# Fixing the order of an expert down stage: even turns of slots and chunks, earlier loads, halves set apart

## The chip, the cores and the metric

The kernel runs on one core of a Trainium2 chip. The metric is the device time of one execution in microseconds (us), as a median of three. All times inside the execution are counted from the start of its profiled span. TensorE is called PE, VectorE DVE, ScalarE ACT; SP is the queue that issues nearly all loads.

## The reference, cut to what matters

Two transformer blocks on 256 tokens of width 1024, all in float32. The stage that changes lies on the seam between them: the down projection of 16 experts (32 tokens each), their gated sum into the residual, and the first feed-forward network of the second block (width 2816), which needs the norm of that residual.

```python
y = jnp.einsum('becf,efd->becd', hid, w_down) * gate[..., None]
x = x + jnp.zeros_like(h).at[bidx, idx].add(y)          # end of block one
# block two, first layer:
h = x + 0.5 * swiglu(rms_norm_2(x, ffn1_norm[0]), ffn1_gate[0], ffn1_up[0], ffn1_down[0])
```

## The kernel before, in words

Activations are kept transposed, as `xt`: eight chunks of 128 features by 256 tokens. The expert down projection goes by **slots**: slot c makes chunk c of the residual. In a slot, eight `y` steps (16 matmuls each, one weight tile of 1 MB each, `in_wd`) make four groups of four experts; each group is copied from PSUM by ACT (`ys`, L1299) and scattered onto the tokens by one `moe` matmul (`sc`, L1304). After the fourth, DVE adds the sum to the residual (`x`, L1310) and ACT and DVE split the chunk into a high and a low part (`xs`), since weights and activations are multiplied as three fp32r products (`mm3`, L478 to L480).

The scale of the norm is a factor per token, so the gate and up projections can begin before the norm is known: as soon as chunk c of the residual is there, 22 **units** (`u`, c, j) multiply it with its rows of the gate and up weights, six matmuls each, and add the result to a partial sum `Pt` (copied by ACT for c = 0, L1323, added by DVE after, L1325). Chunk 7's units come in `first_ffn` (`gate_up`), where the norm's scale (`fin1`, `fin2`, the chain of small DVE operations L561 and L466 to L473) is applied to `Pt` (`evac`) and the down matmuls follow (`down`, `dn`).

The units' weights come in three tiles a chunk (`in_f0g` twice 1 MB for eight units each, `in_f0h` 0.75 MB for six). Each is split on chip in two column halves: ACT writes `wh` (L401), DVE writes `wl` (L402). `slices()` (L306) gives the order of `y`, `sc`, `x` and units: units begin two `y` steps (`LAG`) into slot 1 and are spread over the steps. The same list sets the order of the loads: a unit weight stands `EARLY` = 2 `y` tiles ahead of the step that needs it. `pump` (L376) issues loads while buffers are free: four `raw` ones, and those of a `ring` of 17 that `hold` leaves. The ring also holds the residual, `xs` (two), `Pt` (six), the expert outputs (two) and a pair for each split weight. PSUM tiles of units rotate over the three banks of `pb`.

The order in which instructions stand on an engine is made by a scheduler that goes by priority and its own estimates; only where `behind` binds two instructions is their order fixed. In this stage before, nothing binds them.

Of the kernel before, what the change touches and what calls it, by code (L numbers as in the profile page):

```python
# [32 lines left out]
NF = 22  # L33
RING, RAW, T1, T2 = 17, 4, 10, 10
WARM = (12, 32)
LAG, EARLY = 2, 2
# [202 lines left out]
def _body(tc, nc, const, ringp, work, psum, a, out):  # L239
# [3 lines left out]
    st = {"turn": 0, "ring": 0, "raw": 0, "next": 0, "hold": 0, "la": 2, "late": 0, "gate": None}  # L243
# [62 lines left out]
    def slices():  # L306
# [15 lines left out]
        yield sc  # L322
        yield ("x", 7)
        yield from units[n:]
# [17 lines left out]
    for j in range(NF):  # L342
        if j % 8 == 0:
            add_gs(7, j // 8)
        if j >= 3 and (j - 3) % 2 == 0:
            d0 += add(a["ffn1d0"][len(d0):len(d0) + 1], 1, 1)
    d0 += add(a["ffn1d0"][len(d0):11], 11 - len(d0), 1)
# [28 lines left out]
    def pump():  # L376
        while st["next"] < len(stream):
            if st["raw"] < RAW:
                fetch()
            elif not kinds[st["next"]] and st["ring"] + 2 * any(kinds[i] for i in raw) < RING - st["hold"]:  # L380
# [96 lines left out]
    def mm3(ps, wh, wl, x, first, last):  # L477
        PE.matmul(ps, lhsT=wl, rhs=x[:, 1], start=first, stop=False, skip_group_check=True)  # L478
        PE.matmul(ps, lhsT=wh, rhs=x[:, 0], start=False, stop=False, skip_group_check=True)  # L479
        PE.matmul(ps, lhsT=wh, rhs=x[:, 1], start=False, stop=last, skip_group_check=True)  # L480
# [7 lines left out]
    class Parts:  # L488


        def __init__(self, name):
            self.half = [ralloc([128, 4, 2, 256], F32R, name) for _ in range(2)]

        def __getitem__(self, c):
            return self.half[c // 4][:, c % 4]
# [7 lines left out]
        def part(self, k, c, n):  # L503
            h = self.half[c // 4]
# [12 lines left out]
    class Norm:  # L517


        def __init__(self, g, parts=True, late=0):  # L520
# [3 lines left out]
            if parts:  # L524
                self.x = Parts("xs")
# [53 lines left out]
        def free(self):  # L579
            rfree(2)  # L580
# [501 lines left out]
    n2 = Norm(None, parts=False)  # L1082
# [181 lines left out]
    def slice_steps():  # L1264


        norm, Pt, py, ys, macc = None, [], {}, {}, {}

        def unit(c, j):
# [11 lines left out]
        for op in slices():  # L1281
            if op[0] == "y":
# [5 lines left out]
                w = raw[k].rearrange("p (k g n) -> p k g n", k=4, g=4)  # L1288
                for c in range(4):
                    for g in range(4):  # L1290
                        e = 4 * q + g
                        h = HT[e // 8][:, e % 8].rearrange("p h j s -> p (h j) s")
                        PE.matmul(py[s, q][32 * g:32 * g + 32], lhsT=h[:, 4 * i + c], rhs=w[:, c, g],  # L1293
                                  start=i == 0 and c == 0, stop=i == 1 and c == 3, skip_group_check=True,
                                  tile_position=(0, 32 * g))
                done(k)
                if i == 1:
                    ys[s, q] = t1("ys")[:, :128]
                    S.activation(ys[s, q], py.pop((s, q)), AF.Copy)  # L1299
            elif op[0] == "sc":  # L1300
                _, s, q = op
                if q == 0:
                    macc[s] = pa("moe", (128, 256))
                PE.matmul(macc[s], lhsT=ys.pop((s, q)), rhs=SC[q // 2][:, q % 2],  # L1304
                          start=q == 0, stop=q == 3, skip_group_check=True)
            elif op[0] == "x":
                c = op[1]
                if norm is None:
                    norm = Norm(vc("ffn1n", 0, 8))
                V.tensor_tensor(xt[:, c], macc[c], xt[:, c], op=OP.add)  # L1310
                norm.chunk(c)
                if c == 0:
                    st["hold"], st["la"], st["late"] = 6, 1, 0
                if c == 7:
                    rfree(2)
            else:
                _, c, j = op
                p = unit(c, j)
                if c == 0:
                    if j % 4 == 0:  # L1320
                        Pt.append(ralloc([128, 4, 2, 256], F32, "Pt"))
# [398 lines left out]
```

## Time and profile before

| what | value |
|---|---|
| median of three executions | 1592.27 us (1589.86 to 1592.68) |
| the profiled execution, its own time | 1591.57 us |
| its span | 1589.8 us |
| PE busy | 1445.0 us, 91% of the span |
| DVE busy | 949.6 us, 60% |
| ACT busy | 660.6 us, 42% |
| mean bandwidth of loads | 252 GB/s |

Busy time of PE is modelled, since matmuls overlap; the distance from one matmul's start to the next says more. A window gives its length, the busy time of PE, PE's weight loads (PEld), DVE, ACT and GpSimd (POOL) with their instructions, the granted share of PE's full clock (2.4 GHz), the busy share of the DMA engines, and GB/s. The span has stages: up to 200 us the first mixer, to 474 us the expert gate and up projections, which load 1 MB tiles without a break, from 474 to 729 us the slots, to 820 us the first feed-forward network, and then dense stages of the second block.

### The profile page before, as it was taken

What the parts mean: (1) busy time and instruction counts of PE and PEld (TensorE: products, weight loads), DVE (VectorE), ACT (ScalarE), POOL (GpSimd) and SP (SyncE); (2) the same over time, 40 slices, a digit from 0 to 9 for tenths busy, and PEclk for the clock granted to TensorE, in tenths of its full rate; (3) what the DMA queues carried; (4) which work ended last, traced back from release to release, by engine and by line L of the source; (5) the groups of instructions that cost most, each with busy time, mean ns of one, the idle gap of its engine ahead of it and who ended that gap; (6) DMA issues with size and microseconds to landing.
All of it is one profiled execution on the core that took longest, in us unless ns stands there. A gap on an engine that the chain in (4) does not pass through costs nothing.

```text
span 1589.8 us, 27418 instructions
## 1 busy us (share of the span) xinstructions
PE 1445.0 (91%) x11576; PEld 1150.3 (72%) x11576; DVE 949.6 (60%) x1716; ACT 660.6 (42%) x1152; POOL 6.1 (0%) x11
## 2 busy tenths in 40 slices
PE   9999986666666988898999999999999999999997
PEld 8987721001014877777999998888888899988886
DVE  7976520000000467769968877776867749877673
ACT  6445220000001522115556756554645537665462
POOL 0000000000000000000000000000000000000000
PEclk9999997767667999998999999999999999999999
DMA  7546799999999889884653635545554634636540
GB/s 295 196 137 229 304 397 421 421 421 421 421 422 420 342 323 353 328 356 161 231 203 120 240 142 207 207 159 186 189 209 162 229 133 149 246 124 216 181 159 27
DMA packets 59451, 400.82 MB, mean 252 GB/s; under 512 B 6592, under 2 KB 9792, under 8 KB 12480
## 3 DMA queue, kind: packets, MB, share of 16 engines
q1 hardware_dynamic: 59184, 398.93, 65.8%
q8 instruction: 91, 1.49, 0.4%
q14 instruction: 32, 0.26, 0.0%
q10 hardware_dynamic: 144, 0.14, 0.0%
HBM read 397.99 MB, written 1.05 MB: 251 GB/s over the span
## 4 chain that ended last, share of the span: by engine, by line
PE 70%; DMA 18%; DVE 8%; ACT 3%; issue 1%; DVEq 0%; SPq 0%; ACTq 0%
PE gu L485 15%; DMA w<-in_we 15%; PE gu L486 8%; PE dn L485 8%; PE dn L486 4%; PE y L1293 3%; DVE wl L402 3%; PE gu L478 3%; DMA w<-in_wd 3%; PE gu L479 2%; PE gu L480 2%; ACT wh L401 2%; PE acc L479 2%; PE acc L478 1%; PE acc L480 1%; PE gu L1232 1%
## 5 line engine op out<-in xcount | busy, mean ns | idle before, releaser
L402 DVE TENSOR_TENSOR wl<-w,wh 128x1024 fp32r<-128x1024 f32 (+1 forms) x369 | 435.7, 1204 | 56.8 <-ACT wh L401 49.4
L401 ACT ACTIVATE wh<-w 128x1024 fp32r<-128x1024 f32 (+2 forms) x369 | 364.7, 1037 | 26.2 <-PE dn L485 14.9
L485 PE MATMUL gu<-xs,wh 128*128 128x512 f32 x1056 | 371.7, 395 | 0.0
L486 PE MATMUL gu<-xs,wl 128*128 128x256 f32 x1056 | 294.8, 279 | 0.0
L1232 PE MATMUL gu<-w,xin 128*32 128x512 f32 x1024 | 183.0, 808 | 68.4 <-DMA w<-in_we 68.2
L485 PEld LDWEIGHTS gu<-xs,wh 128*128 128x128 f32 x1056 | 197.9, 188 | 45.8
L486 PEld LDWEIGHTS gu<-xs,wl 128*128 128x128 f32 x1056 | 199.4, 189 | 0.2
L485 PE MATMUL dn<-hx,wh 128*128 128x512 f32 x528 | 186.6, 395 | 0.0
L1232 PEld LDWEIGHTS gu<-w,xin 128*32 128x32 f32 x1024 | 25.8, 123 | 203.7 <-DMA w<-in_we 184.7
L1238 DVE TENSOR_TENSOR hid<-sg,gu 64x512 f32<-64x512 f32 x16 | 11.0, 690 | 250.3 <-ACT sg L1237 250.3
L486 PE MATMUL dn<-hx,wl 128*128 128x256 f32 x528 | 147.5, 279 | 0.0
L478 PE MATMUL gu<-xs,wl 128*128 128x256 f32 x352 | 107.1, 304 | 18.6 <-DVE wl L402 18.4
L485 PEld LDWEIGHTS dn<-hx,wh 128*128 128x128 f32 x528 | 99.0, 188 | 23.1
L1325 DVE TENSOR_TENSOR Pt<-gu,Pt 128x512 f32<-128x512 f32 x132 | 89.9, 690 | 41.1 <-PE gu L480 39.5
L479 PE MATMUL gu<-xs,wh 128*128 128x256 f32 x352 | 101.4, 288 | 0.0
L480 PE MATMUL gu<-xs,wh 128*128 128x256 f32 x352 | 101.4, 288 | 0.0
L486 PEld LDWEIGHTS dn<-hx,wl 128*128 128x128 f32 x528 | 99.7, 189 | 0.0
L1237 ACT ACTIVATE sg<-gu 64x512 f32<-64x512 f32 x16 | 9.4, 590 | 213.0 <-PE gu L1232 213.0
L1293 PE MATMUL y<-w,hidT 128*32 128x128 f32 x2048 | 79.3, 292 | 13.6 <-DMA w<-in_wd 13.6
L478 PEld LDWEIGHTS gu<-xs,wl 128*128 128x128 f32 x352 | 68.8, 196 | 29.3 <-issue 24.6
L1391 DVE TENSOR_TENSOR fz<-gu,fl 128x256 f32<-128x256 f32 x132 | 55.2, 420 | 57.3 <-ACT fl L1390 57.0
L1390 ACT ACTIVATE fl<-gu 128x256 f32<-128x256 f32 x132 | 49.4, 376 | 95.7 <-PE gu L486 95.4
(397 smaller groups left out, 2529.7 us busy)
## 6 DMA issues: line engine op xcount, KB each, us to landing
w<-in_we SPq DMA_DIRECT2D x128, 1024.0 KB, 19.8
w<-in_wd SPq DMA_DIRECT2D x64, 1024.0 KB, 8.3
w<-in_ffn2gu SPq DMA_DIRECT2D x44, 1024.0 KB, 5.0
w<-in_ffn1d SPq DMA_DIRECT2D x22, 1024.0 KB, 4.8
w<-in_wm SPq DMA_DIRECT2D x22, 1024.0 KB, 5.0
w<-in_ffn2d SPq DMA_DIRECT2D x22, 1024.0 KB, 5.1
w<-in_ffn1gu SPq DMA_DIRECT2D x22, 1024.0 KB, 4.9
w<-in_f0g SPq DMA_DIRECT2D x16, 1024.0 KB, 6.7
```

The costliest lines, as they stand in the source:

```text
L401: hi = S.activation(wh, raw[i][:, a0:a1], AF.Copy)
L402: lo = V.tensor_tensor(wl, raw[i][:, a0:a1], wh.bitcast(F32), op=OP.subtract)
L478: PE.matmul(ps, lhsT=wl, rhs=x[:, 1], start=first, stop=False, skip_group_check=True)
L479: PE.matmul(ps, lhsT=wh, rhs=x[:, 0], start=False, stop=False, skip_group_check=True)
L480: PE.matmul(ps, lhsT=wh, rhs=x[:, 1], start=False, stop=last, skip_group_check=True)
L485: PE.matmul(ps, lhsT=wh, rhs=x, start=first, stop=False, skip_group_check=True)
L486: PE.matmul(ps[:, 0], lhsT=wl, rhs=x[:, 1], start=False, stop=last, skip_group_check=True)
L1232: PE.matmul(pg[32 * g:32 * g + 32], lhsT=xin[k // 4][:, k % 4, 32 * e:32 * e + 32], rhs=w[:, g], start=k == 0, stop=k == 7, skip_group_che ...
L1293: PE.matmul(py[s, q][32 * g:32 * g + 32], lhsT=h[:, 4 * i + c], rhs=w[:, c, g], start=i == 0 and c == 0, stop=i == 1 and c == 3, skip_grou ...
L1325: V.tensor_tensor(Pt[j // 4][:, j % 4], p, Pt[j // 4][:, j % 4], op=OP.add)
L1390: S.activation(zl[:, m], p[m][:, 0], AF.Copy)
L1391: V.tensor_tensor(z[:, m], p[m][:, 1], zl[:, m], op=OP.add)
```

## The change: what it does

The list of steps is written anew, and its order is bound on three engines.

1. `in_turn` binds the order on PE (units, `y` steps with their 16 matmuls, `moe`), on ACT (`ys`, the `wh` halves, the copies to `Pt`, `xs`) and on DVE (`x` and `xs`, the `wl` halves, the additions to `Pt`) to the order of the list.
2. The two halves of a unit weight are now two steps of the list (`sp`): they stand apart, each about three units (`SOON`) ahead of the first unit that needs it.
3. Unit weights are loaded four `y` tiles (`EARLY` = 4) ahead of the step of their first half.
4. A `moe` now stands behind the units that follow its last `y` step, not directly behind that step.
5. Room: `xs` takes one ring buffer instead of two, the first six `Pt` tiles lie in small buffers instead of the ring (four ring buffers instead of six), and loads of `in_wd` go to the ring first and to `raw` only when it is full.
6. Units' PSUM tiles rotate over four banks (the three of `pb` and `pc`), and the first three of chunk 7 use `pa`.
7. In `first_ffn`, the additions of chunk 7 are bound behind the norm's chain (`st["gate"]`), the first down weight is split ahead of them, and `down`, `evac` and `gate_up` change places in the loop.

```diff
-LAG, EARLY = 2, 2
+LAG, EARLY, SOON = 2, 4, 3
@@ slices
+        def half_split(n):
+            j = n % NF
+            if j in (0, 4, 8, 12, 16, 19) and n <= len(units):
+                yield ("sp", n // NF, j // 8, j in (4, 12, 19))
+                if n == len(units):
+                    yield ("sp", 7, 0, True)
                 yield ("y", c, k // 2, k % 2)
-                if sc:
+                if sc and sc[2] == 3:
                     yield sc
-                    if sc[2] == 3:
-                        yield ("x", sc[1])
-                sc = ("sc", c, k // 2) if k % 2 else None
+                    yield ("x", sc[1])
+                if (c, k) == (1, 0):
+                    yield ("sp", 0, 0, 0)
                 while n < len(units) and 8 * n < NF * (8 * c - 8 + k + 1 - LAG):
                     yield units[n]
                     n += 1
+                    yield from half_split(n + SOON)
+                if sc and sc[2] < 3:
+                    yield sc
+                sc = ("sc", c, k // 2) if k % 2 else None
...
-        elif op[0] == "u" and op[2] % 8 == 0:
-            order.insert(len(order) - EARLY, ("gs", op[1], op[2] // 8))
+        elif op[0] == "sp" and not op[3]:
+            order.insert(len(order) - EARLY, ("gs", *op[1:3]))
@@ slice_steps
+        def in_turn(first, final, engine="PE"):
+            if engine in last:
+                behind(first, last[engine])
+            last[engine] = final
...
-            p = pb("gu")
-            for m in range(2):
-                mm3(p[:, m], wh[:, j % 8, m], wl[:, j % 8, m], norm.x[c], m == 0, m == 1)
+            p = (bank or (pb, pb, pb, pc)[next(banks) % 4])("gu", (128, 2, 256))
+            ms = [mm3(p[:, m], wh[:, j % 8, m], wl[:, j % 8, m], norm.x[c], m == 0, m == 1) for m in range(2)]
+            in_turn(ms[0][0], ms[1][2])
...
+            if op[0] == "sp":
+                i, h = GS[op[1:3]], op[3]
...
+                hi, lo = cut(i, n * h, n * h + n)
+                in_turn(hi, hi, "ACT")
+                in_turn(lo, lo, "DVE")
...
-                    norm = Norm(vc("ffn1n", 0, 8))
+                    norm = Norm(vc("ffn1n", 0, 8), 1)
@@ first_ffn
-        def gate_up(j):
-            z = Pt[j // 4][:, j % 4]
-            V.tensor_tensor(z, unit(7, j), z, op=OP.add)
+        def gate_up(j, bank=None):
+            i = V.tensor_tensor(Pt[j], unit(7, j, bank), Pt[j], op=OP.add)
+            if st["gate"] is not None:
+                behind(i, st["gate"])
...
+        split(d0[0])
         for j in range(6):
-            gate_up(j)
+            gate_up(j, pa if j < 3 else None)
             if j == 0:
                 norm.fin1(pa)
-        norm.fin2()
-        for j in range(4):
-            evac(j)
+            if j == 3:
+                norm.fin2()
+                evac(0)
+        evac(1)
         for j in range(6, NF):
-            evac(j - 2)
+            down(j - 6)
+            evac(j - 4)
             gate_up(j)
-            down(j - 6)
```

Both programs hold the same matmuls, splits, additions and loads; only their order, buffers and banks differ. Three places show what moved.

**ACT at the seam of slots 0 and 1**, from the fourth `ys` copy on (`ss` is the square of residual chunk 0, `xs` the high part of that chunk, `wh` the halves of the first unit weight). Before:

```order
L1299 ACTIVATE ys<-y 128x128 x4
L545 ACTIVATE ss<-x 128x256
L1299 ACTIVATE ys<-y 128x128 x3
L532 ACTIVATE xs<-x,vec 128x256
L401 ACTIVATE wh_3605<-w_3449 128x1024 x2
L1323 ACTIVATE Pt<-gu 128x512 x5
```

After:

```order
L1337 ACTIVATE ys<-y 128x128 x4
L560 ACTIVATE ss<-x 128x256
L547 ACTIVATE xs<-x,vec 128x256
L416 ACTIVATE wh_3565<-w_3300 128x1024
L1337 ACTIVATE ys<-y 128x128
L1369 ACTIVATE Pt<-gu 128x512
L416 ACTIVATE wh_3565<-w_3300 128x1024
```

The chunk's split and the first half of the weight moved ahead of three copies of slot 1.

**DVE in the middle of the stage**, from the addition of residual chunk 3 on (`wl` are weight halves, one number for each weight). Before:

```order
L1310 TENSOR_TENSOR x<-moe,x 128x256
L402 TENSOR_TENSOR wl_4582<-w_4343,wh_4581 128x768 x2
L533 SCALAR_TENSOR_TENSOR xs<-x,vec,xs 128x256
L1325 TENSOR_TENSOR Pt<-gu,Pt 128x512
L549 TENSOR_TENSOR ss<-ss,sq 128x256
L1325 TENSOR_TENSOR Pt<-gu,Pt 128x512 x5
L402 TENSOR_TENSOR wl_4705<-w_4457,wh_4704 128x1024 x2
L1325 TENSOR_TENSOR Pt<-gu,Pt 128x512 x8
L402 TENSOR_TENSOR wl_4819<-w_4587,wh_4818 128x1024 x2
L1325 TENSOR_TENSOR Pt<-gu,Pt 128x512 x8
```

After:

```order
L1351 TENSOR_TENSOR x<-moe,x 128x256
L548 SCALAR_TENSOR_TENSOR xs<-x,vec,xs 128x256
L564 TENSOR_TENSOR ss<-ss,sq 128x256
L1372 TENSOR_TENSOR Pt<-gu,Pt 128x512 x2
L417 TENSOR_TENSOR wl_4647<-w_4342,wh_4646 128x1024
L1372 TENSOR_TENSOR Pt<-gu,Pt 128x512 x4
L417 TENSOR_TENSOR wl_4647<-w_4342,wh_4646 128x1024
L1372 TENSOR_TENSOR Pt<-gu,Pt 128x512 x4
L417 TENSOR_TENSOR wl_4784<-w_4360,wh_4783 128x1024
L1372 TENSOR_TENSOR Pt<-gu,Pt 128x512 x4
```

Before, both halves of a weight stand right behind the last additions of the units of the weight before; after, three to four additions lie between any two halves.

**DVE after the last residual chunk**, on the way to the norm (`var`, `rt` and `tmp` are the norm's chain; `wl_6124` is the first down weight). Before:

```order
L1310 TENSOR_TENSOR x<-moe,x 128x256
L1325 TENSOR_TENSOR Pt<-gu,Pt 128x512
L533 SCALAR_TENSOR_TENSOR xs<-x,vec,xs 128x256
L549 TENSOR_TENSOR ss<-ss,sq 128x256
L1325 TENSOR_TENSOR Pt<-gu,Pt 128x512 x4
L1337 TENSOR_TENSOR Pt<-gu,Pt 128x512
L561 TENSOR_SCALAR var<-ssT 128x2
L1337 TENSOR_TENSOR Pt<-gu,Pt 128x512
L466 TENSOR_SCALAR rt<-var 128x2
L1337 TENSOR_TENSOR Pt<-gu,Pt 128x512
L467 TENSOR_TENSOR tmp<-rt 128x2
```

After:

```order
L1351 TENSOR_TENSOR x<-moe,x 128x256
L548 SCALAR_TENSOR_TENSOR xs<-x,vec,xs 128x256
L564 TENSOR_TENSOR ss<-ss,sq 128x256
L1372 TENSOR_TENSOR Pt<-gu,Pt 128x512 x2
L417 TENSOR_TENSOR wl_6090<-w_5808,wh_6089 128x1024 x2
L1372 TENSOR_TENSOR Pt<-gu,Pt 128x512 x3
L417 TENSOR_TENSOR wl_6124<-w_5828,wh_6123 128x1024 x2
L1384 TENSOR_TENSOR Pt<-gu,Pt 128x512
L576 TENSOR_SCALAR var<-ssT 128x2
L481 TENSOR_SCALAR rt<-var 128x2
L482 TENSOR_TENSOR tmp<-rt 128x2
```

The chain itself is no longer interleaved with additions, but four weight halves now stand ahead of it.

## Rows read from the trace of the kernel before

**Rows 1.** Windows between residual additions: length; five busy times; clock, DMA share, GB/s

```profile
533.09:561.79 28.70, 27.23 (x391) 22.99 (x390) 16.87 (x23) 8.26 (x15) 0.00 (x0) 1.00 0.90 353
...
596.78:628.50 31.72, 28.56 (x397) 24.28 (x397) 22.36 (x31) 7.17 (x12) 0.00 (x0) 1.00 0.91 357
...
660.09:696.53 36.44, 31.57 (x397) 27.14 (x397) 22.92 (x32) 8.64 (x14) 0.00 (x0) 0.91 0.82 312
...
728.64:820.00 91.36, 85.16 (x691) 84.19 (x690) 84.53 (x144) 47.84 (x83) 0.00 (x0) 0.94 0.56 200
```

**Rows 2.** Tile moe, the residual additions: duration in ns min/median/max, first and last start

```profile
L1310 DVE TENSOR_TENSOR x<-moe,x x8: 414/424/425, 493.9 to 728.6; 128x256 f32<-128x256 f32 x8
```

**Rows 3.** Waits of PE's weight loads, 540 to 728 us: total us, times, longest

```profile
PEld gu L478 <- issue: 23.9, 21, 3.1
PEld moe L1304 <- ACT ys L1299: 4.0, 6, 0.7
```

**Rows 4.** Timeline 604 to 610 us: start, length, engine; idle before and releaser

```profile
604.59 2.35 DVE L402 TENSOR_TENSOR wl<-w,wh 128x1024 fp32r<-128x1024 f32 x2
...
605.95 0.36 PE L478 MATMUL gu<-xs,wl 128*128 128x256 f32 x1 [0.37 <-DVE wl L402]
...
606.74 0.28 PE L478 MATMUL gu<-xs,wl 128*128 128x256 f32 x1
...
606.94 2.13 DVE L1325 TENSOR_TENSOR Pt<-gu,Pt 128x512 f32<-128x512 f32 x3
...
607.46 0.28 PE L478 MATMUL gu<-xs,wl 128*128 128x256 f32 x1
...
608.26 1.08 PE L1293 MATMUL y<-w,hidT 128*32 128x128 f32 x32
...
609.28 0.39 PE L478 MATMUL gu<-xs,wl 128*128 128x256 f32 x1
```

**Rows 5.** Timeline 486 to 517 us, slots 0 and 1

```profile
486.68 1.08 PE L1293 MATMUL y<-w,hidT 128*32 128x128 f32 x32 [1.40 <-DMA w<-in_wd]
...
501.68 1.94 PE L1293 MATMUL y<-w,hidT 128*32 128x128 f32 x32 [0.64 <-DMA w<-in_wd]
...
513.93 0.50 ACT L532 ACTIVATE xs<-x,vec 128x256 fp32r<-128x256 f32 x1
...
516.68 0.39 PE L478 MATMUL gu<-xs,wl 128*128 128x256 f32 x1
```

**Rows 6.** Timeline 733 to 744 us, the norm's chain to the first down matmul

```profile
733.46 0.15 DVE L561 TENSOR_SCALAR var<-ssT 128x2 f32<-128x2 f32 x1
...
739.91 0.69 PE L569 MATMUL rbT<-cst,rt 128*128 128x128 f32 x2 [2.06 <-DVE rt L473]
...
743.87 1.01 PE L478 MATMUL dn<-hx,wl 128*128 128x256 f32 x3 [3.28 <-ACT hx L514]
```

**Rows 7.** The page's costliest groups, ACT's halves: count, busy us, mean ns, idle before

```profile
L401 ACT ACTIVATE wh<-w 128x1024 fp32r<-128x1024 f32 (+2 forms) x369 | 364.7, 1037 | 26.2 <-PE dn L485 14.9
```

**Rows 8.** Window over the `y` steps of slot 1, columns as in rows 1

```profile
499.10:508.60 9.50, 6.96 (x98) 4.76 (x98) 0.00 (x0) 0.31 (x2) 0.00 (x0) 0.50 1.01 420
```

**Rows 9.** Timeline near 727 us: one scatter matmul and the unit behind it

```profile
727.13 0.60 PE L1304 MATMUL moe<-scat,ys 128*128 128x256 f32 x2
...
727.58 0.38 PE L478 MATMUL gu<-xs,wl 128*128 128x256 f32 x1
```

**Rows 10.** The loads' queue, 540 to 728 us: what it waited for

```profile
SPq L373 <- PE y L1293: 93.5, 23, 9.1
```

**Rows 11.** Window 700 to 720 us, columns as in rows 1

```profile
700.00:720.00 20.00, 17.98 (x250) 15.26 (x250) 14.16 (x20) 6.69 (x10) 0.00 (x0) 1.00 0.99 400
```

**Rows 12.** Timeline near 175 us: a norm's chain with nothing between

```profile
175.44 0.16 DVE L561 TENSOR_SCALAR var<-ssT 128x2 f32<-128x2 f32 x1 [1.44 <-PE ssT L556]
...
177.01 0.16 DVE L473 SCALAR_TENSOR_TENSOR rt<-tmp,rt 128x2 f32<-128x2 f32 x1
```

**Rows 13.** Waits in the whole stage, 474 to 732 us: ACT's halves for their load

```profile
ACT wh L401 <- DMA w<-in_f0g: 0.2, 1, 0.2
```

More of the change, by code (lines that the diff above doesn't have):

```diff
@@ L240, in _body @@
     V, S, PE, G = nc.vector, nc.scalar, nc.tensor, nc.gpsimd
-    st = {"turn": 0, "ring": 0, "raw": 0, "next": 0, "hold": 0, "la": 2, "late": 0, "gate": None}
+    st = {"turn": 0, "ring": 0, "raw": 0, "next": 0, "hold": 0, "la": 2, "late": 0, "gate": None, "sliced": False}
     def ralloc(shape, dt, name, tag="ring"):
@@ L321, in slices @@
                     n += 1
+                    yield from half_split(n + SOON)
+                if sc and sc[2] < 3:
+                    yield sc
+                sc = ("sc", c, k // 2) if k % 2 else None
         yield sc
         yield ("x", 7)
-        yield from units[n:]
+        for n in range(n, len(units)):
+            yield units[n]
+            yield from half_split(n + 1 + SOON)
     order, DS, GS = [], {}, {}
@@ L341, in _body @@
     d0 = []
-    for j in range(NF):
-        if j % 8 == 0:
+    for j in range(6, NF + 6):
+        if j in (8, 16):
             add_gs(7, j // 8)
-        if j >= 3 and (j - 3) % 2 == 0:
+        if j % 2 == 0:
             d0 += add(a["ffn1d0"][len(d0):len(d0) + 1], 1, 1)
-    d0 += add(a["ffn1d0"][len(d0):11], 11 - len(d0), 1)
     def add_ffn(n, l):
@@ L377, in pump @@
         while st["next"] < len(stream):
-            if st["raw"] < RAW:
+            if st["sliced"] and not kinds[st["next"]] and st["ring"] < RING - st["hold"]:
+                fetch(tag="ring")
+            elif st["raw"] < RAW:
                 fetch()
-            elif not kinds[st["next"]] and st["ring"] + 2 * any(kinds[i] for i in raw) < RING - st["hold"]:
+            elif not st["sliced"] and not kinds[st["next"]] and st["ring"] + 2 * any(kinds[i] for i in raw) < RING - st["hold"]:
                 fetch(tag="ring")
@@ L488, in _body, with __init__ @@
     class Parts:
-        def __init__(self, name):
-            self.half = [ralloc([128, 4, 2, 256], F32R, name) for _ in range(2)]
+        def __init__(self, name, n=2):
+            self.half = [ralloc([128, 4, 2, 256], F32R, name) for _ in range(n)]
         def __getitem__(self, c):
-            return self.half[c // 4][:, c % 4]
+            return self.half[c // 4 % len(self.half)][:, c % 4]
         def lo(self, c, n=1):
@@ L517, in _body, with __init__ @@
     class Norm:
-        def __init__(self, g, parts=True, late=0):
+        def __init__(self, g, parts=2, late=0):
             self.g = g
@@ L579, in free @@
         def free(self):
-            rfree(2)
+            rfree(self.parts)
     def wpair(i):
@@ L1264, in slice_steps, with unit @@
     def slice_steps():
-        norm, Pt, py, ys, macc = None, [], {}, {}, {}
-        def unit(c, j):
+        norm, Pt, py, ys, macc, last = None, [], {}, {}, {}, {}
+        banks = iter(range(1 << 30))
+        def in_turn(first, final, engine="PE"):
+            if engine in last:
+                behind(first, last[engine])
+            last[engine] = final
+        def unit(c, j, bank=None):
             i = GS[c, j // 8]
@@ L1308, in slice_steps @@
                 if norm is None:
-                    norm = Norm(vc("ffn1n", 0, 8))
[L1310 to L1313, printed above, removed]
+                    norm = Norm(vc("ffn1n", 0, 8), 1)
+                    st["hold"] -= 1
+                i = V.tensor_tensor(xt[:, c], macc[c], xt[:, c], op=OP.add)
+                hi, lo = norm.split(c)
+                in_turn(i, lo, "DVE")
+                in_turn(hi, hi, "ACT")
+                norm.square(c)
                 if c == 7:
```

67 lines of the change are left out of this document (43 added, 24 removed).

## The prediction

> **What bounds the kernel now.** First come the windows cut at the residual additions [rows 1]. The additions start at 493.9 us and end at 728.6 us [rows 2], and the stretches between them are what the change works on: 28.7 us for slot 2, 31.7 us for a slot in the middle, 36.4 us for a bad one. From 533.1 to 728.6 us six slots take 195.5 us, 32.6 us each. In none of them is an engine full: in the middle one PE is busy 28.6 of 31.7 us, DVE 22.4, the DMA engines 0.91 of the time. So the slots go by waits. The waits of PE say which [rows 3]: before the first matmul of a unit, 23.9 us in 21 waits, three for a slot, one for each unit weight. The profile puts them down to "issue", but the timeline shows what ends them [rows 4]: PE's matmul at 605.95 us is released by the `wl` half that DVE began at 604.59 us, behind the additions of the units before. Scatter matmuls add 4.0 us of waits for `ys` [rows 3].
>
> The seam of slots 0 and 1 is bound otherwise. There PE waits for the loads: the `y` steps of the sixth and the twelfth tile of the stage start at 486.68 and 501.68 us, each released by its load [rows 5], six tiles in 15.0 us, 2.50 us for a tile of 1 MB. But the high part of residual chunk 0, which was ready for it soon after 493.9 us, is made at 513.93 us, since it stands on ACT behind copies of later `y` steps, and the first unit starts at 516.68 us [rows 5].
>
> Behind the slots, the first feed-forward network runs from the last addition to 820 us, 91.4 us [rows 1]. PE is idle twice there, 2.06 us before the norm's transpose and 3.28 us before the first down matmul at 743.87 us [rows 6].
>
> **The change part by part.** Matmuls, splits, additions and loads stay the same in number and size, so only waits and order count. I go by X0 to X7, the residual additions.
>
> *Start, to X1.* Tile 13 of the stage, the one whose `y` step stands before the first unit in the new order, lands one tile after the twelfth: 501.7 + 2.5 = 504.2 us. Chunk 0 comes later than before, since a unit weight now precedes its last tiles: the last lands at 486.68 + 5 x 2.50 = 499.2 us, and with a `y` step and a scatter behind it X0 is at about 500.8 us instead of 493.9. The addition (0.42 us), the high part (0.50) and a first half on ACT (1.0) and DVE (1.2) [rows 2, 4, 5, 7] bring it to 503.9 us. So the first unit starts behind the thirteenth tile's `y` step, at about 505.3 us, 11 us sooner. To X1 it is 17 units, six `y` steps and four scatters. A unit is 0.72 us (606.74 to 607.46 us), a `y` step with its two changes of operand 1.1 us (the last unit's end at 608.18, the next unit at 609.28) [rows 4], a scatter 0.45 us (727.13 to 727.58) [rows 9]: 12.2 + 6.6 + 1.8 = 20.6 us. PE's granted clock is 0.50 there, 1.2 GHz [rows 8], behind the waits for loads; a step at 501.68 us takes 1.94 us instead of 1.08 [rows 5]. Some 5 us of work at that level cost 2.5 us more. X1 comes at about 528 us instead of 533.1: 5 us. The loads for it (7.75 tiles, 19.4 us from 504.2) land at 523.6 us and do not set it.
>
> *Slots, X1 to X7.* With no wait a slot is 22 units, eight `y` steps and four scatters: 15.8 + 8.8 + 1.8 = 26.4 us. From the other side, the middle slot less its share of the unit waits (23.9 us over 188 us, 4.0 us) is 27.7 us. The loads of a slot are 10.75 tiles, 26.9 us at 2.50 us. These two are nearly equal, so a little of either will show; I take 27.4 us. The waits go because each half now has two or three units between itself and its first use, some 1.5 to 2.5 us for a half of 1.2 us. What hides the halves is slack on DVE: 22 additions at 0.71 us, 6.5 us of halves (four at 1.18, two of three quarters of that size) and 1.3 us for `x`, `xs` and `ss` are 23.4 us of 27.4 [rows 2, 4]. If that cover went, every addition behind would hold a bank; four banks now, instead of three, give it one unit more. `ys` have the units behind their step as cover now; if it fails, it is the 0.7 us a time that a scatter waits at most now [rows 3]. Six slots of 27.4 are 164.4 us: X7 at 692.4 us instead of 728.6, 36.2 us.
>
> Do the loads keep up? The queue waited for `y` steps to free buffers 93.5 us [rows 10]. In mid-stage 15 of the 17 ring buffers were taken (residual 1, expert outputs 2, `xs` 2, `Pt` 6, two pairs 4), which with four raw ones left six for tiles; three are freed. In the new order the first weight of each chunk is itself held until the first `y` of a slot has freed a buffer, five loads earlier, and all tiles behind it wait with it on SP; at 27 us a slot that leaves tiles six to eight us ahead of their use.
>
> On the pace of loads, the window from 700 to 720 us holds 400 GB/s with PE busy 18 and DVE 14 of 20 us [rows 11]. The Trainium skill ("DMA: Bandwidth & Descriptors", Bandwidth) puts the HBM limit for a core near 358 GB/s and says that it binds loads from HBM. By that, a slot's loads would take an estimated 31.5 us and the slots would hardly shrink. The trace does not agree, with its 400 GB/s here and 420 before compute sets in [rows 8]; the 11.27 MB of a slot (10.75 tiles of 1.048 MB) take 28.2 us at the lower of the two.
>
> *Behind X7.* DVE now does, after X7: the addition, `xs` and `ss` (1.8 us with ACT's part), two additions (1.4), two halves (2.4), three additions (2.1), two halves of the first down weight (2.4), one addition (0.7): 10.8 us, then the chain. Alone it takes 177.01 + 0.16 - 175.44 = 1.7 us [rows 12], where before it took from 733.46 to 739.85 us, 6.4 us, with additions between [rows 6]. So the scale is there 12.5 us after X7, against 11.2 us before. From there to the first down matmul it was 4.0 us [rows 6]; three additions in between take 2.1 us beside the transpose and its copy, so I take 4.4 us: 16.9 us after X7 against 15.2. PE has then done seven units of chunk 7 where before it had done nine, since the transpose stands on PE between the fourth and fifth: 1.4 us. And units 8 and later wait for halves that DVE makes late: 1 us. Together 4 us slower (bounds: 4.6 us faster, if DVE's pieces are done ahead and the chain starts 4.8 us after X7 as before; 8 us slower, with one down step of 24 matmuls at half clock, 2.9 us more than at 0.12 us each [rows 4], and 1 us more of halves).
>
> *Sum.* 36.2 - 4.2 = 32 us less: 1591.6 - 32 = 1559.6 us from the profiled execution, which is 0.7 us under the median shown. I say 1560.
>
> **The rivals.**
>
> *The queue of loads sets the slot.* If the held first weight lets the DMA engines run dry for 2 to 3 us each slot, a slot is 29.7 us, X7 is at 706 us, 22 us gained, 4 lost: 1573 us. For it: the slots hold 312 to 357 GB/s [rows 1], where loads alone hold 420 [rows 8]. Against it: DMA share 0.99 at 400 GB/s in the last window of the slots [rows 11].
>
> *Loads beside compute are capped.* If 357 GB/s [rows 1] is a ceiling and not the result of buffers freed late, a slot takes 11.27 MB / 357 = 31.6 us and only 6 us are gained: 1586 us. The 400 GB/s speak against it [rows 11]. This is the case of the page named above.
>
> *Slower: ACT and DVE blocked by the fixed order.* With halves bound ahead of `ys` and `Pt`, a weight that lands late holds every copy behind it, and PE with them, where before the scheduler had put halves last. 21 weights pass; at 1.5 us each the gain is gone (32 / 21), at 2 us the time is 1602 us. Against it: the halves waited 0.2 us in all for their loads [rows 13], and weights are asked for earlier now. What such an order costs shows in slot 1 before, where `xs` stood some 20 us behind copies on ACT [rows 5].
>
> *Everything fits, the tail too.* Slots of 26.6 us from X1 at 526 us, and the norm's chain early: X7 at 685.6 us, 4.6 us more behind: 1544 us.
>
> **How the numbers follow.** Forecast 0.62, with its own range 1552 to 1570; queue 0.17; cap 0.06; slower 0.06; everything fits 0.09. The range that leaves out the cap, the slow case and the ends of the rest is 1549 to 1576 us. No change within 0.2% (3.2 us, about what three executions tell apart) needs a cap or a blocked queue of just the right size: 0.02, from the cap and the slow case. Faster 0.93, slower 0.05.
>
> **What would show it.** In the profile after: the first unit near 505 us; X1 near 528 and X7 near 692 us; waits before units for a weight half down from 24 us to under 5; DMA share above 0.95 between 530 and 690 us; the first down matmul some 17 us after X7, and its stage some 95 us long. The forecast is wrong if slots stay above 30 us, if ACT or DVE show waits for unit weights of more than 1 us each, or if PE's idle time before units is now put down to loads.

## The result and the profile after

| | before | after |
|---|---|---|
| median | 1592.47 us (1589.86 to 1597.14, four executions) | 1556.01 us (1555.72 to 1556.49, four) |
| span of the profiled execution | 1589.8 us | 1554.1 us |
| residual additions, first and last (X0, X7) | 493.9, 728.6 us | 501.3, 691.6 us |
| last down matmul of the stage ends | 820.2 us | 784.3 us |

The ratio is 0.9768 (95% interval 0.9745 to 0.9791): 36 us, all of them won by the end of the stage (820.2 - 784.3 = 35.9).

The windows between residual additions of the changed kernel, columns as in [rows 1]; first X0 to X1, then the slots from X1 to X6 (two left out) and X6 to X7, and at the end the six slots together:

```profile
501.28:527.59 26.31, 24.55 (x368) 21.06 (x369) 7.72 (x9) 16.78 (x29) 0.00 (x0) 0.95 1.01 419
527.59:554.73 27.14, 27.14 (x398) 23.84 (x397) 18.89 (x26) 9.72 (x17) 0.00 (x0) 1.00 1.01 417
554.73:582.76 28.03, 27.28 (x398) 23.85 (x397) 21.79 (x31) 7.19 (x12) 0.00 (x0) 1.00 1.01 419
...
637.59:664.73 27.14, 27.14 (x398) 23.84 (x397) 21.80 (x32) 7.19 (x12) 0.00 (x0) 1.00 1.00 411
664.73:691.59 26.86, 26.86 (x374) 23.89 (x373) 21.71 (x31) 7.19 (x12) 0.00 (x0) 1.00 0.86 339
...
527.59:691.59 164.00, 162.79 (x2354) 143.12 (x2353) 127.78 (x181) 45.66 (x77) 0.00 (x0) 1.00 0.99 404
```

Two columns are full at once: PE is busy 162.8 of 164.0 us at full clock, and the DMA engines 0.99 of the time. A slot is 27.3 us where it was 32.6 [rows 1].

The waits of PE's weight loads, 540 to 700 us (total us, times, longest), against [rows 3]:

```profile
PEld gu L493 <- issue: 5.8, 29, 0.2
PEld y L1329 <- issue: 5.6, 17, 0.3
...
PEld gu L493 <- DVE wl L417: 1.0, 1, 1.0
```

From X1 to X7 no wait for a half is left (the one of 1.0 us lies behind X7); 29 waits of 0.2 us are the change of operand behind a `y` step. The timeline shows why, against [rows 4]: between the half that DVE begins at 612.84 us and its first use PE has three units and a further `y` step to do, where before it had none.

```profile
611.64 1.28 DVE L1372 TENSOR_TENSOR Pt<-gu,Pt 128x512 f32<-128x512 f32 x2
611.95 1.08 PE L1329 MATMUL y<-w,hidT 128*32 128x128 f32 x32
612.84 1.21 DVE L417 TENSOR_TENSOR wl<-w,wh 128x1024 fp32r<-128x1024 f32 x1
612.96 0.39 PE L493 MATMUL gu<-xs,wl 128*128 128x256 f32 x1
...
613.18 0.28 PE L494 MATMUL gu<-xs,wh 128*128 128x256 f32 x1
...
613.98 1.88 DVE L1372 TENSOR_TENSOR Pt<-gu,Pt 128x512 f32<-128x512 f32 x3
```

The seam of slots 0 and 1, against [rows 5]: DVE begins the first half at 503.53 us, and only a `y` step at half clock (1.94 us at 501.58) and one at full clock (1.08) stand before the first unit, at 505.16 us instead of 516.68.

```profile
501.28 0.42 DVE L1351 TENSOR_TENSOR x<-moe,x 128x256 f32<-128x256 f32 x1 [28.46 <-PE moe L1343]
...
501.58 1.94 PE L1329 MATMUL y<-w,hidT 128*32 128x128 f32 x32 [0.34 <-DMA w<-in_wd]
...
503.53 1.23 DVE L417 TENSOR_TENSOR wl<-w,wh 128x1024 fp32r<-128x1024 f32 x1 [0.46 <-ACT wh L416]
...
504.15 1.08 PE L1329 MATMUL y<-w,hidT 128*32 128x128 f32 x32 [0.64 <-DMA w<-in_wd]
...
505.16 0.19 PEld L493 LDWEIGHTS gu<-xs,wl 128*128 128x128 f32 x1 [0.20 <-issue]
```

Behind X7, against [rows 6]: the two halves of the first down weight (698.59 us) stand ahead of the chain, which now takes 1.7 us in one piece; PE waits 3.95 us for it.

```profile
698.59 2.34 DVE L417 TENSOR_TENSOR wl<-w,wh 128x1024 fp32r<-128x1024 f32 x2
...
701.46 0.14 DVE L576 TENSOR_SCALAR var<-ssT 128x2 f32<-128x2 f32 x1
...
703.01 0.16 DVE L488 SCALAR_TENSOR_TENSOR rt<-tmp,rt 128x2 f32<-128x2 f32 x1
...
703.32 0.66 PE L584 MATMUL rbT<-cst,rt 128*128 128x128 f32 x2 [3.95 <-DVE rt L488]
```

The first down matmul starts at 708.0 us, 16.4 us after X7 (before 15.2), and the stage ends 92.7 us after X7 (before 820.2 - 728.6 = 91.6).

### The profile page after: what moved, and what is told of

Same layout as the page of the kernel before. It is cut to its first block, busy times and chain, and to the rows that moved or that the text cites. A ratio compares the mean times of both kernels' runs of the same rounds, so it can differ in the third digit from the quotient of the medians.

```text
span 1554.1 us, 27418 instructions
## 1 busy us (share of the span) xinstructions
PE 1431.4 (92%) x11576; PEld 1142.6 (74%) x11576; DVE 946.4 (61%) x1716; ACT 661.1 (43%) x1152; POOL 6.1 (0%) x11
## 4 chain that ended last, share of the span: by engine, by line
PE 69%; DMA 21%; DVE 6%; ACT 2%; issue 1%; SPq 0%; DVEq 0%; ACTq 0%
PE gu L500 16%; DMA w<-in_we 15%; PE gu L501 8%; PE dn L500 8%; DMA w<-in_wd 5%; PE dn L501 4%; PE y L1329 3%; PE gu L493 2%; DVE wl L417 2%; PE gu L494 2%; PE gu L495 2%; PE acc L494 2%; PE acc L493 1%; PE acc L495 1%; PE gu L1247 1%; PE dn L493 1%
## 5 line engine op out<-in xcount | busy, mean ns | idle before, releaser
L416 ACT ACTIVATE wh<-w 128x1024 fp32r<-128x1024 f32 (+1 forms) x369 | 365.9, 1037 | 25.7 <-PE dn L500 14.9
L501 PEld LDWEIGHTS gu<-xs,wl 128*128 128x128 f32 x1056 | 199.1, 189 | 0.2
L1329 PE MATMUL y<-w,hidT 128*32 128x128 f32 x2048 | 74.1, 289 | 13.2 <-DMA w<-in_wd 13.1
L1329 PEld LDWEIGHTS y<-w,hidT 128*32 128x32 f32 x2048 | 55.5, 115 | 30.1 <-DMA w<-in_wd 13.6
```

Of the source, the lines that this page charges most:

```text
L416: hi = S.activation(wh, raw[i][:, a0:a1], AF.Copy)
L501: PE.matmul(ps[:, 0], lhsT=wl, rhs=x[:, 1], start=False, stop=last, skip_group_check=True)
L1329: ms.append(PE.matmul(py[s, q][32 * g:32 * g + 32], lhsT=h[:, 4 * i + c], rhs=w[:, c, g], start=i == 0 and c == 0, stop=i == 1 and c == 3, ...
```

## The experiments

All medians are set against runs of the kernel before on the same chip; the intervals of the ratios reach some 3 us to either side, so smaller differences between two of these runs are not told apart. Slots are means over X1 to X7. Two parts of the change were not tried apart: which of the three engines needs its order bound, and the later place of the `moe`.

### How far ahead a half must stand

```diff
-LAG, EARLY, SOON = 2, 4, 3
+LAG, EARLY, SOON = 2, 4, 0
```

> SOON = 0: each half of a unit weight stands in the list right before the first unit that needs it; the bound order, the room, the early loads and the four banks stay. Theory (the slots were bound by PE waiting for halves, and the three units between a half and its use are what removes that): DVE reaches a half only after the additions of the units before it, 0.7 us behind PE, and then takes 1.2 us, so PE waits about 1 us before each of the six halves of a slot. Slots of 33 us instead of 27.3, residual addition 7 near 728 us, 1591 us in all (1575 to 1605), and the waits of PE's weight loads name DVE wl or issue with more than 25 us between 530 and 700 us. Rival (the gain came from loads and room, or from binding the order at all): slots stay under 29 us and the time under 1567 us.

Measured: 1669.07 us, ratio 1.0485 (1.0467 to 1.0503). Slots are 42.8 us. The same order on three engines, with the halves three units nearer to their use, is 113 us slower than the changed kernel and 77 us slower than before. The window over the six slots and PE's waits in them:

```profile
544.62:801.50 256.88, 187.70 (x2348) 158.60 (x2348) 132.04 (x181) 46.03 (x77) 0.00 (x0) 0.92 0.64 237
```

```profile
PE gu L493 <- DVE wl L417: 69.2, 36, 2.7
```

36 halves, 1.9 us each, where 1 us was expected. The waits are 11.5 us a slot; PE's busy time grows from 162.8 to 187.7 us for the same matmuls, since its granted clock falls to 0.92 on the mean, another 4.2 us a slot. Together 15.7 us, against the 15.5 that a slot grew. Why a half costs 1.9 us shows around one of them:

```profile
600.93 2.00 ACT L416 ACTIVATE wh<-w 128x1024 fp32r<-128x1024 f32 x2
...
601.63 0.69 DVE L1372 TENSOR_TENSOR Pt<-gu,Pt 128x512 f32<-128x512 f32 x1 [1.66 <-PE gu L495]
602.24 1.22 DVE L417 TENSOR_TENSOR wl<-w,wh 128x1024 fp32r<-128x1024 f32 x1
...
603.60 0.36 PE L493 MATMUL gu<-xs,wl 128*128 128x256 f32 x1 [2.01 <-DVE wl L417]
```

PE has finished a unit, and DVE, bound to do that unit's addition first (0.69 us from 601.63), only then makes the half (1.22 us); PE starts at 603.60, 2.01 us late. ACT's half, two of which take 2.00 us from 600.93, is not what is waited for. That holds for nearly all of them; DVE's halves waited for ACT's twice in the six slots, and the other 34 stand directly behind an addition:

```profile
DVE wl L417 <- ACT wh L416: 8.4, 2, 6.9
```

The theory named this chain, but 0.7 and 1.2 us add up to 1.9, not to about 1.

```diff
-LAG, EARLY, SOON = 2, 4, 3
+LAG, EARLY, SOON = 2, 4, 1
```

> SOON = 1: a half stands one unit (0.72 us) ahead of the unit that needs it, in the bound order. With no distance each half cost PE about 2 us (six a slot, slots of 43 us instead of 27.3). Theory (a half takes 1.0 us on ACT and 1.2 on DVE one after the other, so a distance covers its own length of PE's work, and what is not covered is waited for): one unit takes 0.7 to 1.1 us off each wait, slots of 35 to 39 us, 1610 to 1635 us. Rival (only the order matters, any distance will do, as the bound copies no longer stand between a half and its unit): slots under 29 us, 1555 to 1566 us.

Measured: 1602.97 us, ratio 1.0059 (1.0037 to 1.0082), slots 33.8 us. PE's waits over the six slots:

```profile
PE gu L493 <- DVE wl L417: 28.8, 24, 2.1
```

4.8 us a slot, and PE's busy time of 173.6 us adds 1.8: the 6.5 us that a slot grew. On the mean one unit takes 1.1 us off each of the 36 waits, the upper end of what the theory gave: most became 0.6 to 0.7 us shorter, and 12, which have a `y` step in the distance too, are gone. The theory's picture of a half, ACT's part and then DVE's, is not what is covered: ahead of DVE's part stands the addition, as above; three units, 2.1 us, cover the 1.9. The time came out 7 us under the range because 2.4 us a slot of lost clock came back too (187.7 - 173.6 us of busy time, over six slots).

### The order without binding

```diff
-            if engine in last:
+            if False:
                 behind(first, last[engine])
```

> No binding of the order in the slots: the list, with halves three units ahead, early loads, room and banks stay, but the scheduler places the instructions of PE, ACT and DVE by its own estimates, which brings the two halves of a weight together again at places and moves the residual additions. Theory (the list alone does not do it; the binding turns it into even slots): slots 28 to 30 us, 1561 to 1573 us, waits of PE's weight loads for halves of 5 to 15 us in the slots. Rival (spacing and room do all, binding nothing): 1554 to 1558 us, slots 27.2 us. Rival (binding is what costs, as the run with no distance hints): faster than 1553 us.

Measured: 1590.76 us, ratio 0.9980 (0.9964 to 0.9996), slots 32.5 us. All three theories missed: the list, the room and the early loads without the binding are worth next to nothing. On DVE the scheduler puts the halves of a weight side by side again (the 2.35 us), right behind a residual addition and ahead of that chunk's `xs`, 12 us later:

```profile
624.92 0.42 DVE L1351 TENSOR_TENSOR x<-moe,x 128x256 f32<-128x256 f32 x1 [8.90 <-PE moe L1343]
625.27 2.35 DVE L417 TENSOR_TENSOR wl<-w,wh 128x1024 fp32r<-128x1024 f32 x2
...
637.46 0.48 DVE L548 SCALAR_TENSOR_TENSOR xs<-x,vec,xs 128x256 fp32r<-128x256 f32 x1
```

and the loads' queue waits for DVE's halves, which free its buffers, so that PE waits for loads too (waits of SP's queue and of PE, 500 to 725 us).:

```profile
SPq L386 <- DVE wl L417: 133.5, 15, 13.6
...
PE y L1329 <- DMA w<-in_wd: 14.1, 10, 2.9
PE gu L493 <- DVE wl L417: 9.6, 6, 1.7
```

The queue's wait for DVE's halves is not new: it was 85.9 us in 540 to 728 us before the change, which [rows 10] leave out, and is 68.7 us in 530 to 690 us of the changed kernel.

### Room, early loads, spacing of the pair, banks

```diff
@@ room taken back
-        st["hold"], ... = 7, 0, 0, True
+        st["hold"], ... = 10, 0, 0, True
-                    norm = Norm(vc("ffn1n", 0, 8), 1)
+                    norm = Norm(vc("ffn1n", 0, 8), 2)
-                    if j < 6:
-                        Pt.append(t2("Pt"))
...
+                    if j % 4 == 0:
+                        four = ralloc([128, 4, 2, 256], F32, "Pt")
```

> The room is taken back: the parts of the residual take two ring buffers and all 22 partial sums lie in six ring buffers, three buffers fewer for tiles under way; order, spacing, early loads and banks stay. Theory (the loads of a slot, 26.9 us at 2.50 us a tile, are nearly as long as PE's 26.4 us, so with four ring buffers instead of seven for tiles the queue stops for y steps and does not catch up): slots 28.5 to 29.5 us, 1563 to 1571 us, a DMA share under 0.95 in the slots. Rival (seven tiles were more than was needed; PE alone sets the slot): slots 27.3 us, 1554 to 1558 us.

Measured: 1572.15 us, ratio 0.9875 (0.9857 to 0.9893), slots 29.6 us. The room is worth 16 us. The window over the six slots, and PE's waits (530 to 690 us):

```profile
532.40:710.24 177.84, 166.39 (x2354) 145.59 (x2353) 127.83 (x181) 45.65 (x77) 0.00 (x0) 0.98 0.93 371
```

```profile
PE y L1329 <- DMA w<-in_wd: 8.6, 9, 2.0
```

The DMA share falls to 0.93 and PE waits for `y`'s tiles, never for halves.

```diff
-LAG, EARLY, SOON = 2, 4, 3
+LAG, EARLY, SOON = 2, 2, 3
```

> EARLY = 2: unit weights are loaded two tiles of the down weight ahead of the step of their first half instead of four. Theory (loads run six to eight us ahead of their use in the slots, so 5 us less is just covered, and the start gains a little since chunk 0's last tiles are not preceded by two unit weights): 1552 to 1560 us, first waits of ACT for a unit weight small. Rival (loads are as near to the limit as PE, so a weight that comes two tiles later holds ACT and all behind it): 1 to 2 us for each of 21 weights, 1575 to 1595 us.

Measured: 1555.50 us, ratio 0.9765 (0.9748 to 0.9783), slots 27.1 us. Asking for weights two tiles sooner changes nothing that shows.

```diff
-            if j in (0, 4, 8, 12, 16, 19) and n <= len(units):
-                yield ("sp", n // NF, j // 8, j in (4, 12, 19))
-                if n == len(units):
-                    yield ("sp", 7, 0, True)
+            if j in (0, 8, 16) and n <= len(units):
+                yield ("sp", n // NF, j // 8, False)
+                yield ("sp", n // NF, j // 8, True)
```

> The second half of a unit weight stands directly behind the first, still three units ahead of the first use. Theory (what counts is that a half is begun a few units ahead; four banks hold the units whose additions stand behind 2.4 us of halves): within 5 us of the changed kernel, 1556 to 1561 us, slots 27.3 to 28.1. Rival (it is the even spacing of halves that counts, since 2.4 us of halves in one piece hold the additions and so the banks): a wait of 0.5 us or more at each of 21 weights, slots over 28.8 us, 1566 us or more.

Measured: 1558.45 us, ratio 0.9786 (0.9771 to 0.9800), 2.4 us over the changed kernel, which is less than can be told apart. Its slots are 27.6 us, five of them 27.2 or less and one of 30.8 with a wait of 2.0 us for a `y` tile; no wait for a half is over 0.4 us. So it is the distance that counts, not that the two halves stand apart.

```diff
-            p = (bank or (pb, pb, pb, pc)[next(banks) % 4])("gu", (128, 2, 256))
+            p = (bank or pb)("gu", (128, 2, 256))
```

> The PSUM tiles of the units rotate over three banks as before the change, in the slots and in the first feed-forward network but for its first three units; all else stays. Theory (an addition that stands behind a half of 1.2 us on DVE holds its bank, and PE runs up to three units ahead of the additions at the four-bank spacing): PE waits for additions about 0.3 to 0.6 us behind each of 42 halves, slots 28.5 to 30 us, 1564 to 1574 us. Rival (three banks cover a half of 1.2 us, 1.7 units): 1555 to 1558 us.

Measured: 1555.72 us, ratio 0.9766 (0.9748 to 0.9785), slots 27.3 us. The fourth bank is worth nothing here; the theory fell.

### What bounds a slot now

```diff
 def unit(c, j, bank=None):
-            ms = [mm3(p[:, m], wh..., wl..., norm.x[c], m == 0, m == 1) for m in range(2)]
+            ms = [(PE.matmul(p[:, m], lhsT=wl[:, j % 8, m], rhs=norm.x[c][:, 1], ...),
+                   PE.matmul(p[:, m], lhsT=wh[:, j % 8, m], rhs=norm.x[c][:, 0], ...)) for m in range(2)]
```

> The third product of each unit (high weights by the high part of the residual) is left out in the slots and in the first feed-forward network, which takes a third of PE's work from the units, 22 x 0.24 = 5.3 us of a slot's 27.14 us; loads, splits and additions stay. Theory (PE, 27.14 us, and the loads, 11.27 MB at 417 GB/s = 27.0 us, bind the slot together): slots stay at 26.9 to 27.2 us with a DMA share of 1.0 and PE now waiting for y's loads, residual addition 7 near 690 us. Rival (PE alone binds, and the loads have room to go faster): slots of 24 us, bound by DVE's 21.8 us and its waits, residual addition 7 near 671 us.

Measured in one execution: 1549.78 us; X7 at 689.34 us, slots 27.3 us. The window over the six slots, and PE's waits from 500 to 725 us:

```profile
525.77:689.34 163.57, 137.01 (x2090) 114.89 (x2089) 123.13 (x182) 45.55 (x77) 0.00 (x0) 0.97 0.99 408
```

```profile
PE y L1331 <- DMA w<-in_wd: 29.6, 23, 2.8
```

PE has 26 us less to do and the slots last as long, with the DMA engines at 0.99 and PE now waiting for `y`'s tiles. So loads alone bind a slot at 27.3 us, and PE alone at 27.1, as in the windows of 27.14 us above, in which it never waits. The stage ends 8.3 us sooner, 6.1 of them behind X7, where the products are left out too (86.6 us instead of 92.7); the stages behind it took 2.2 us more.

### The stretch behind X7

Four runs try to start the down matmuls sooner. The first calls the norm's chain ahead of chunk 7's units and splits the first down weight behind it:

```diff
-        split(d0[0])
+        norm.fin1(pa)
         for j in range(6):
             gate_up(j, pa if j < 3 else None)
-            if j == 0:
-                norm.fin1(pa)
             if j == 3:
                 norm.fin2()
                 evac(0)
+                split(d0[0])
```

> The norm's chain ahead: its sum over features is called before the units of chunk 7, and the first down weight is split behind the norm's scale instead of ahead of the chain. On DVE 3.0 us (two halves and one addition) leave the way to the chain, and stand behind it. Theory (the work that DVE must do before the first down matmul sets the start of the down matmuls, and it is only put in another order): the scale 2.8 us sooner, the first down matmul within 1 us of 16.4 us after residual addition 7, time 1555 to 1557.5 us. Rival (the chain's place sets it): first down matmul 2.5 to 3 us sooner, 1552.5 to 1553.5 us.

The second makes the low halves of that weight on GpSimd (in `cut`, for this weight alone):

```diff
-        lo = V.tensor_tensor(wl, raw[i][:, a0:a1], wh.bitcast(F32), op=OP.subtract)
+        lo = G.tensor_tensor(wl, raw[i][:, a0:a1], wh.bitcast(F32), op=OP.subtract)
```

> The low halves of the first down weight are made by GpSimd, idle in this stage, instead of by DVE: 2.35 us of DVE's work between residual addition 7 and the norm's chain go away, all else stays. Theory (DVE, busy 15.6 of 16.4 us there, sets the first down matmul): it comes 2 to 2.4 us sooner, 1553 to 1554.5 us. Rivals: GpSimd takes so long for a half (over 5 us each) or slows DVE so much that the first down matmul waits for it: 1556 us or more; or PE's work, not DVE's, sets the stage: 1556 us.

The third and fourth take two halves into the last slot, both with the chain ahead: those of the first down weight, or those of chunk 7's first weight.

```diff
                 yield ("y", c, k // 2, k % 2)
+                if (c, k) in ((7, 6), (7, 7)):
+                    yield ("d0", k - 6)            # third
+                    yield ("sp", 7, 0, k == 7)     # fourth
...
```

> Both halves of the first down weight are split in the last slot, behind its last two y steps, where DVE is busy 21.7 of 26.9 us, and the norm's chain stands ahead of the units of chunk 7 (as in the run with the chain ahead). Its load is issued at 673 us in the changed kernel and is there in time. So 2.35 us of DVE's work and 2 us of ACT's leave the stretch behind residual addition 7, in which DVE is busy 15.6 of 16.4 us and PE waits for it. Theory (DVE's work there sets the stage's start): the first down matmul 13.5 to 14.5 us after residual addition 7 instead of 16.4, the stage 90 to 91 us instead of 92.6, residual addition 7 no later than 693.5 us, 1552.5 to 1555 us. Rival (the stage is as long as PE's work and the clock it gets, and an early start is given back, as in the run with the chain ahead; or the two halves delay the last slot by 1 to 2 us): 1555.5 to 1557.5 us.

> In the run with the first down weight split in the last slot, DVE stood 4.7 us behind ACT, which waited for that weight's load, and residual addition 7 came 4.4 us later than in the changed kernel; but its stage was 89.1 us instead of 92.6. Here the weight that is split in the last slot is the first one of chunk 7, whose load is issued at 670.6 us and lands some 8 us later, well ahead of the y steps in question; the first down weight is split behind the chain, which stands ahead of chunk 7's units. The loads keep their order. Theory (DVE's 2.35 us taken out of the stretch behind residual addition 7 shorten the stage, if nothing bound waits for a load): residual addition 7 no later than 692.7 us counted from an addition 0 at 501.3 us, the first down matmul 13 to 14.5 us after it, the stage 90 to 91.3 us, 1553.5 to 1555 us. Rival (what is won at the first down matmul is given back, since DVE is full up to the end of the stage with the splits of further weights): stage 92 us or more, 1555.5 us or more.

| run | median, ratio (interval) | X7 | first down matmul after X7 | stage's end after X7 | end after X0 |
|---|---|---|---|---|---|
| changed kernel | 1556.01 | 691.6 | 16.4 | 92.7 | 283.0 |
| chain ahead | 1556.46, 0.9761 (0.9743 to 0.9779) | 693.0 | 14.9 | 92.0 | 281.4 |
| GpSimd | 1555.57, 0.9758 (0.9740 to 0.9776) | 692.3 | 16.5 | 91.7 | 281.1 |
| down weight in slot 7 | 1557.85, 0.9778 (0.9760 to 0.9796) | 697.5 | 14.2 | 89.1 | 282.5 |
| chunk 7's weight in slot 7 | 1556.18, 0.9765 (0.9747 to 0.9783) | 694.5 | 12.6 | 89.7 | 282.7 |

X0 itself lies at 501.3 to 504.1 us in these five executions, though nothing ahead of it was changed, so the last column counts from X0. None is faster than the changed kernel by what can be told apart, though three start the down matmuls 1.5 to 3.8 us sooner after X7. What was won came back as three different waits. With the chain ahead, PE waits later, at unit 8, for a half that DVE, now without a gap, reaches only 0.8 us sooner after X7 (windows of that run, 712 to 720 us):

```profile
712.00:716.00 4.00, 2.05 (x18) 1.84 (x16) 4.00 (x9) 2.20 (x6) 0.00 (x0) 1.00 0.00 0
716.00:720.00 4.00, 3.27 (x20) 3.30 (x21) 4.00 (x8) 4.00 (x7) 0.00 (x0) 0.74 0.00 0
```

PE is busy half of the first 4 us, DVE all of them, and in the next 4 us the granted clock is 0.74. With the down weight in slot 7, ACT waited for its load (first line), the bound `wl` and all behind it stood, and the last slot took 31.3 us instead of 26.9, with X7 4.0 us later than the theory allowed:

```profile
688.81 1.79 ACT L418 ACTIVATE wh<-w 128x1024 fp32r<-128x1024 f32 x2 [5.56 <-DMA w<-in_ffn1d]
689.90 1.23 DVE L419 TENSOR_TENSOR wl<-w,wh 128x1024 fp32r<-128x1024 f32 x1 [4.65 <-ACT wh L418]
```

With chunk 7's weight there, the scheduler put ACT's halves of the first down weight, which nothing binds, ahead of the bound second half. They waited 3.88 us for a buffer that a `wl` frees (the `wh` pair at 687.54), and DVE 2.60 us behind that:

```profile
687.54 2.01 ACT L416 ACTIVATE wh<-w 128x1024 fp32r<-128x1024 f32 x2 [3.88 <-DVE wl L417]
...
689.61 1.78 ACT L416 ACTIVATE wh<-w 128x1024 fp32r<-128x1024 f32 x2
690.69 1.23 DVE L417 TENSOR_TENSOR wl<-w,wh 128x1024 fp32r<-128x1024 f32 x1 [2.60 <-ACT wh L416]
```

Whether that order with those two copies bound as well would keep X7 at 691.6 us and the stage of 89.7 was not tried; it stays open.

## Why the prediction was right, and where it was wrong

The time was forecast as 1560 us and came out at 1556.0, inside the forecast's own range.

1. *Start.* X0 at 500.8 us (measured 501.3), first unit at 505.3 (505.16), X1 at 528 (527.6). The last of these was right by luck. The 2.5 us for half clock were put on the units and steps behind the first unit. But the half clock had ended by then; only the `y` step at 501.58 us still had it (1.94 us instead of 1.08), and all that follows runs at 1.00:

```profile
507.00:512.00 5.00, 4.40 (x61) 3.67 (x62) 1.23 (x1) 3.21 (x7) 0.00 (x0) 1.00 1.01 421
```

From the first unit to X1 it took 22.4 us, 1.8 more than the 20.6 of work: 0.8 us are waits for two of `y`'s tiles, though the prediction held that loads do not set this stretch, and some 0.1 us more went into each of six `y` steps (see 2).

2. *Slots.* 27.4 us was forecast, 27.3 measured, X7 at 692.4 against 691.6 us. The two bounds were nearly equal, as said, but both were a little low. PE without a wait needs 27.14 us, not 26.4. The term that was short is the `y` step: the first matmul behind it holds PE for 0.22 us instead of 0.12 (612.96 to 613.18 us), so a step costs 1.2 us and not 1.1, 0.8 us over eight. The loads take 27.3 us, not 26.9, in the run with a product less.
3. *Which part does it.* The prediction put the slots' gain down to the distance between a half and its use. That holds, in the fixed order: 42.8, 33.8 and 27.3 us a slot with 0, 1 and 3 units. It had not said that the binding alone, without distance, makes the kernel slower by 77 us, nor that distance in the list without binding gives nothing. Early loads and the fourth bank, which it counted on its side, are worth nothing that shows, each taken back by itself.
4. *The rivals.* The queue of loads is the one that the room holds off: with three buffers fewer, slots take 29.6 us, near its 29.7, and the time is 1572 us, near its 1573, though from fewer buffers and not from a held first weight. The cap at 357 GB/s is refuted by 411 to 419 GB/s from X0 to X6 with PE full from X1 on. The Trainium skill ("DMA: Bandwidth & Descriptors", Bandwidth) says that its limit near 358 GB/s binds loads from HBM, which the prediction took up, but also that this is a core's share when both cores of a pair stream; here one core runs, and the trace shows no such limit. The slower rival was a weight that lands late and holds the bound copies on ACT and DVE. It did not come in the changed kernel; the run with the down weight in slot 7 shows it, with 5.56 us of ACT waiting for the load and 4.4 us more for the slot. The runs with no distance and one unit are slow by another way (1.9 and 0.8 us a half, the addition ahead of the half on DVE), which the prediction did not name.
5. *Behind X7, the step that was mis-sized.* "Together 4 us slower" was 1.1 us slower. The start of the down matmuls was nearly right: 1.2 us later against X7 than before (1.7 forecast). PE had also done fewer matmuls by then, 69 in 16.41 us against 79 in 15.36, 1.2 us of them at 0.12 us each (1.4 forecast). But it made most of them good in the 16 us behind, 114 against 105. The windows suggest why. Before, 744 to 760 us:

```profile
744.00:748.00 4.00, 4.00 (x19) 3.98 (x20) 4.00 (x11) 2.52 (x8) 0.00 (x0) 0.50 0.00 0
748.00:752.00 4.00, 3.13 (x21) 2.87 (x21) 4.00 (x8) 1.08 (x3) 0.00 (x0) 0.74 0.19 31
...
744.00:760.00 16.00, 15.13 (x105) 14.85 (x106) 15.94 (x30) 9.23 (x19) 0.00 (x0) 0.81 0.51 180
```

and after, the stretch to the first down matmul and that behind it:

```profile
691.59:708.00 16.41, 10.69 (x69) 9.70 (x68) 15.55 (x32) 8.16 (x13) 0.00 (x0) 0.81 0.56 193
...
703.30:708.04 4.74, 4.25 (x19) 3.87 (x19) 4.74 (x10) 1.55 (x4) 0.00 (x0) 0.50 0.39 161
...
708.00:724.00 16.00, 13.82 (x114) 13.47 (x113) 14.56 (x25) 9.24 (x15) 0.00 (x0) 0.98 0.05 7
```

The kernel before ran its first down matmuls at half clock (0.50, then 0.74), behind PE's waits of 2.06 and 3.28 us. The changed kernel's low clock, behind a wait of 3.95 us, lies ahead of the first down matmul: PE does 19 matmuls at 0.50 there, while DVE and ACT still make that matmul's input `hx` (done at 707.4 us), and the matmuls behind it run at 0.98. The prediction charged only the new order for half clock, in its upper bound, and did not credit it with what the old order lost. That the clock's place makes up the whole difference was read from two executions, not tested by itself. The 1 us put down for late halves shows as two waits in the same stretch, 1.02 us of unit 8 at 716.07 us and 1.16 us of a down matmul at 720.34 us, and the 114 already contain them.

## What to carry to other kernels

Fixing the order on several engines pays only with distance in it: each producer must stand ahead of its use by its own length and that of what is bound ahead of it on its engine (here 1.2 us for a half and 0.7 us for an addition), counted in the consumer's work, and nothing bound may stand behind a load that can still be on its way. When slots even out, look whether two engines are full at once (here PE and the loads, both at 27 us); then taking work from one of them gives nothing. And look where the granted clock is low: a stall ahead of work that others wait for can cost more than its own length, and one ahead of work with room to spare less, as the two executions behind X7 suggest.

## What the runs showed of the hardware

A small instruction of DVE can stand still for one of GpSimd. In the run with GpSimd's halves, the first step of the norm's chain that follows `var`, 128x2 elements, took 2.10 us instead of 0.17, and ended with GpSimd's second instruction (696.60 + 5.51 = 702.11 us):

```profile
696.60 5.51 POOL L417 TENSOR_TENSOR wl<-w,wh 128x1024 fp32r<-128x1024 f32 x2 [607.57 <-ACT wh L416]
...
699.85 0.15 DVE L576 TENSOR_SCALAR var<-ssT 128x2 f32<-128x2 f32 x1
700.03 2.10 DVE L481 TENSOR_SCALAR rt<-var 128x2 int32<-128x2 int32 x1
702.16 0.16 DVE L482 TENSOR_TENSOR tmp<-rt 128x2 f32<-128x2 f32 x1
```

The additions before it, with one input from PSUM, ran on at their usual 0.6 to 0.7 us. The Trainium skill ("SBUF — State Buffer", SBUF: two separate sides) has DVE and GpSimd share a pair of ports by a lock that is held for a whole instruction; the trace agrees, with 2.10 us. So the 2.35 us that GpSimd took from DVE came back as 1.9 us in the chain. GpSimd needed 3.2 and 2.3 us for its two halves, DVE 1.2 for one.

Loads held 411 to 419 GB/s from X0 to X6, 163 us, most of it beside a full PE and a DVE busy 21.8 of 27.1 us.
